# A two-layer decoder trunk on one core: layer 0 in one hand-ordered region, first transfers by k-tile, squares of the norm on GpSimd, retention angles behind the norm

## The chip, the cores and the metric

The kernel runs on one core of one Trainium2 chip. The time is device time of one execution in microseconds. The kernel before took 431.51 us (median of three runs, 431.0 to 431.7); the changed kernel is timed against it on the same chip.

## The reference

A causal trunk of two layers over 256 positions of width 1024, in fp32. Cut to what matters here:

```python
def reference(x, mem, positions, ...):
    cos, sin = rotary_tables(positions, attn_inv)      # 32 frequencies: heads of layer 0
    rcos, rsin = rotary_tables(positions, ret_inv)     # 128 frequencies: retention, layer 1
    mem_n = rms_norm(mem, mem_norm_g)
    x = even_layer(x, mem_n, cos, sin, ...)            # layer 0
    x = odd_layer(x, mem_n, rcos, rsin, ...)           # layer 1
    return rms_norm(x, final_norm_g)

def even_layer(x, ...):
    h = rms_norm(x, norm_g)
    (nq, nkc, nvc, nks, nvs, nkw, nvw, ng, nz, mq, mk, mv, mz, eq, ez) = _split(h @ w_in, EVEN_SPLITS)
    # a_out: sparse attention (compressed, selected, window), b_out: block attention, m_out: memory attention
    y = jnp.concatenate([a_out * jax.nn.silu(nz), b_out * jax.nn.silu(mz), m_out * jax.nn.silu(ez)], axis=-1) @ w_out
    return x + y
```

Layer 1 projects to retention queries, keys, values and gates and to a second memory attention, and maps back in the same way.

## The kernel before

Every product of fp32 matrices is made of three matmuls of a rounded high part and a low part (high by high, high by low, low by high). Weights come from memory in *units* of 128 x 1024 (512 KB; the compression's are 128 x 560), through a ring of six `raw` buffers. For each unit ScalarE casts the high part `whi` (L165), VectorE subtracts the low part `wlo` (L173), both into rings of four; 1.2 us of VectorE and 1.0 us of ScalarE per unit of 1024. TensorE works on the projections one after another: 24 matmuls per unit.

The row norm of `x` is not applied before the projections: x times gain is split (`xh`, `xl`, buffers named `big`), and 1/rms (`rstd0`) is multiplied into the results and the rotary tables later. So the first matmuls need only x and weights, while squares, their sum, and the reciprocal root run beside them.

The start, in order: the first projection (sparse keys, L402 to L411) runs k-tile by k-tile, eight of them. For each, ScalarE casts the weight (`split`, L144) and x (`gain_cast`, L342), VectorE makes the two low parts (L145 and `gain_low`, L346), and TensorE runs six matmuls of 512 columns (L409) into banks s0 and s1. `square(q)` (L399) squares a quarter of x on ScalarE. Then come the compression's projection (four units of 560, 12 matmuls of 280 columns each), the sparse queries (four units of 1024), the sparse gates (`project_turned`, which take banks s0 and s1 again), the block keys, and so on.

Beside the projections run small tasks, written as generators and advanced by `turn()` once per step of a projection (a *slot*, counted from the compression's first). `until(AT[..])` holds a task up to a slot. Four of them matter: `tables` (rotary angles of layer 0, on VectorE), `norms` (adds the squares on GpSimd, L491 and L492; sums over rows by a matmul, L497; reciprocal root by small steps on VectorE, `rsqrt_steps`, L132 to L137; spreads it over the partitions by a matmul, L504; scales the tables on ScalarE, L510 to L518), `tables1` (the angles of layer 1's retention, L483 to L463 on GpSimd, sine and cosine on ScalarE, L465 to L469), and `compressed` (values cast on ScalarE, L747, transposed by TensorE into bank o, L754 and L755).

Inside `tc.manual_schedule(engines=...)` the named engines run their instructions in the order in which the program emits them; outside, a planner orders them. An engine is in order in any case: an instruction that waits holds back all behind it. Before, the start consists of several such regions, some for the sync engine and ScalarE alone, so that the planner may interleave VectorE's, TensorE's and GpSimd's work of neighbouring parts.

## Time and profile before

| | |
|---|---|
| median of three runs | 431.51 us |
| the profiled execution's own time | 431.38 us |
| its span, first to last instruction | 429.6 us |
| TensorE busy | 417.7 us, 97% |
| VectorE busy | 308.1 us, 72% |
| ScalarE busy | 242.3 us, 56% |
| GpSimd busy | 18.1 us, 4%, nearly all between 13 and 33 us |
| granted TensorE clock | 0.998 |

How to read it: PE is TensorE, PEld its weight loads, DVE VectorE, ACT ScalarE, POOL GpSimd; SPq and ACTq are queues that issue transfers. A row of the timeline has start and duration in us, engine, line, operation, what is written and read, and in brackets the idle time before it and who ended it. The busy time is cut into stretches where it is used, since the engines' shares differ between the first 30 us and the rest.

### The profile page before, as it was taken

Reading aid. Unit: us, or ns where it says so; the run is one execution under the profiler, and the core shown is the slowest. Engines: PE = TensorE matmul, PEld = TensorE weight load, DVE = VectorE, ACT = ScalarE, POOL = GpSimd, SP = SyncE. Lnnn points to the kernel's source line nnn. Section 1 sums busy time; section 2 is a strip of 40 time slices with the busy share of each in tenths; the row PEclk is TensorE's granted clock in tenths of the full one; section 3 lists DMA queues with packets and bytes.
Section 4 is the critical chain, followed back from the end, with each engine's and each line's share of the span. In section 5 each row is a group of like instructions: output and inputs, shape, how many; then the busy total and the mean of one; then the engine's idle time right before and its main releaser. Section 6 shows DMA issues by size and latency. Waiting matters only on the chain.

```text
span 429.6 us, 7028 instructions
## 1 busy us (share of the span) xinstructions
PE 417.7 (97%) x2622; PEld 361.1 (84%) x2622; DVE 308.1 (72%) x667; ACT 242.3 (56%) x452; POOL 18.1 (4%) x24
## 2 busy tenths in 40 slices
PE   7889999999999999999999999999999999999994
PEld 5678988777899987879999988889998888888883
DVE  3997988779697585668677674677887467695634
ACT  5759375677876584746356344456444445545703
POOL 0690000000000000000000000000000000000000
PEclk9999999999999999999999999999999999999999
DMA  8786554344666453535444446545454554655102
GB/s 275 269 283 211 199 179 129 135 148 155 215 235 214 133 154 124 163 115 182 156 171 163 153 152 186 196 169 195 148 164 164 178 190 176 205 178 186 69 0 98
DMA packets 21937, 73.18 MB, mean 170 GB/s; under 512 B 2704, under 2 KB 3728, under 8 KB 21904
## 3 DMA queue, kind: packets, MB, share of 16 engines
q1 hardware_dynamic: 21328, 72.04, 50.9%
q10 hardware_dynamic: 576, 0.71, 0.7%
q8 instruction: 20, 0.33, 0.3%
q14 instruction: 13, 0.11, 0.1%
HBM read 71.69 MB, written 1.05 MB: 169 GB/s over the span
## 4 chain that ended last, share of the span: by engine, by line
PE 88%; DVE 7%; DMA 1%; issue 1%; ACT 1%; SPq 0%; DVEq 0%
PE pj L244 23%; PE pj L246 22%; PE pj L245 22%; PE o L116 4%; DVE wlo L173 2%; PE s L116 2%; PE s L323 2%; PE t L323 2%; DMA raw<-in_w 1%; PE s L244 1%; PE s L246 1%; PE s L245 1%; PE tr L244 1%; PE tr L246 1%; PE tr L245 1%
## 5 line engine op out<-in xcount | busy, mean ns | idle before, releaser
L173 DVE TENSOR_TENSOR wlo<-raw,whi 128x1024 fp32r<-128x1024 f32 (+1 forms) x118 | 142.6, 1211 | 62.8 <-ACT whi L165 60.7
L165 ACT CAST whi<-raw 128x1024 fp32r<-128x1024 f32 (+1 forms) x118 | 121.6, 1036 | 91.9 <-PE pj L246 38.2
L244 PE MATMUL pj<-whi,big 128*128 128x512 f32 (+2 forms) x256 | 97.4, 383 | 0.0
L245 PE MATMUL pj<-wlo,big 128*128 128x512 f32 (+2 forms) x256 | 96.2, 376 | 1.1 <-DVE wlo L173 1.1
L246 PE MATMUL pj<-whi,big 128*128 128x512 f32 (+2 forms) x256 | 95.9, 375 | 0.0
L244 PE MATMUL pj<-big,whi 128*128 128x256 f32 x256 | 73.5, 287 | 0.0
L246 PE MATMUL pj<-big,wlo 128*128 128x256 f32 x256 | 72.6, 284 | 0.0
L245 PE MATMUL pj<-big,whi 128*128 128x256 f32 x256 | 72.5, 283 | 0.0
L245 PEld LDWEIGHTS pj<-wlo,big 128*128 128x128 f32 x256 | 48.3, 189 | 9.4 <-DVE wlo L173 1.5
L244 PEld LDWEIGHTS pj<-whi,big 128*128 128x128 f32 x256 | 48.2, 188 | 9.3 <-issue 1.5
L246 PEld LDWEIGHTS pj<-whi,big 128*128 128x128 f32 x256 | 48.2, 188 | 8.7
L244 PEld LDWEIGHTS pj<-big,whi 128*128 128x128 f32 x256 | 49.0, 191 | 1.9 <-issue 1.8
L245 PEld LDWEIGHTS pj<-big,whi 128*128 128x128 f32 x256 | 49.0, 191 | 0.1
L246 PEld LDWEIGHTS pj<-big,wlo 128*128 128x128 f32 x256 | 49.0, 191 | 0.0
L608 ACT ACTIVATE p<-p,mx 128x128 f32<-128x128 f32 (+1 forms) x48 | 21.2, 443 | 4.5 <-DVE mx L595 4.4
L244 PE MATMUL pj<-whi,y 128*128 128x512 f32 x42 | 16.9, 407 | 0.0
L246 PE MATMUL pj<-whi,y 128*128 128x512 f32 x42 | 16.4, 391 | 0.0
L245 PE MATMUL pj<-wlo,y 128*128 128x512 f32 x42 | 16.2, 391 | 0.0
L570 DVE TENSOR_SCALAR p<-p,sm 128x256 f32<-128x256 f32 (+1 forms) x48 | 12.7, 322 | 0.6
L568 ACT ACTIVATE p<-p,sm 128x256 f32<-128x256 f32 (+1 forms) x16 | 7.8, 487 | 7.9 <-DVE sm L564 7.5
L595 DVE CUSTOM_DVE_ANT_0 p<-s,cst 128x128 f32<-128x128 f32 (+1 forms) x24 | 7.1, 353 | 5.5 <-PE s L116 5.5
L409 PE MATMUL s<-whi,big 128*128 128x512 f32 x32 | 9.0, 396 | 2.0 <-ACT big L342 1.6
(349 smaller groups left out, 657.9 us busy)
## 6 DMA issues: line engine op xcount, KB each, us to landing
raw<-in_w SPq DMA_DIRECT2D x91, 512.0 KB, 3.8
raw<-in_wout SPq DMA_DIRECT2D x28, 512.0 KB, 3.9
raw<-in_w SPq DMA_DIRECT2D x4, 280.0 KB, 3.5
v<-in_w SPq DMA_DIRECT2D x2, 512.0 KB, 6.1
raw<-in_memT SPq DMA_DIRECT2D x2, 512.0 KB, 3.8
raw<-in_memtok SPq DMA_DIRECT2D x2, 512.0 KB, 4.6
v<-in_xtok SPq DMA_DIRECT2D x2, 512.0 KB, 5.4
v<-in_grow SPq DMA_DIRECT2D x2, 512.0 KB, 7.2
```

Of the source, the lines that this page charges most:

```text
L116: ins = PE.matmul(out, lhs, rhs, start=start, stop=stop)
L165: S.copy(hi, raw)
L173: V.tensor_tensor(lo, raw, hi.bitcast(F32), ALU.subtract)
L244: PE.matmul(ps, lh, rh, start=start, stop=False, skip_group_check=shared)
L245: PE.matmul(ps, lh, rl, start=False, stop=False, skip_group_check=shared)
L246: return PE.matmul(ps, ll, rh, start=False, stop=stop, skip_group_check=shared)
L323: PE.transpose(b[:, i * P : (i + 1) * P], a, ident)
L409: PE.matmul(ps_k[tok], x[:, kt, tok * P : (tok + 1) * P], w, start=kt == 0 and i == 0, stop=kt == KT - 1 and i == 2)
L568: S.activation(p[:, hh, a], p[:, hh, a], AF.Copy, scale=sm[:, hh, tok : tok + 1])
L570: V.tensor_scalar(p[:, hh, a], p[:, hh, a], sm[:, hh, tok : tok + 1], None, op0=ALU.mult)
L595: V.tensor_tensor_reduce(ps[i][:, hh, a], ss[i][hh][:, a], cpak[:, C_CAUSAL + a.start : C_CAUSAL + a.stop], -1.0, 3e38, ALU.add, ALU.min, ...
L608: S.activation(ps[i][:, hh, a], src, AF.Exp, bias=ms[i][:, hh, tok : tok + 1], scale=-1.0 if causal else 1.0, accum_out=ns[i][:, hh, tok : ...
```

## The change

It rewrites how the first part of the program is ordered.

- The whole of layer 0, from the first transfer to its output projection, becomes one region in which all five engines follow the order of emission.
- The first transfers all go through the sync queue, in the order in which k-tiles use them: weight half, x tile, weight half, and so on; ScalarE's queue keeps only the vector of gains. Each later weight of the first projection (128 x 1024) comes as two transfers. (In the diff, the list of `drive` calls is left out where it only loses its indentation.)
- `square(q)` moves from ScalarE to GpSimd as a product of x with itself, and adds up as it goes; it stands at a k-tile's start instead of one pair later.
- `tables` is advanced by hand behind the first two units of the compression, and no longer interleaved with the last k-tiles.
- `tables1` begins at slot 10 instead of 3, takes its first cast on VectorE, and its sines come at slot 14 instead of 10. The sum of squares comes at slot 3 instead of 5, the compression's steps at 15 and 24 instead of 13 and 22.

```diff
--- before.py
+++ after.py
@@ -31,7 +31,7 @@
 BANKS = {"pj": 3, "tr": 1, "t": 1, "s0": 1, "s1": 1, "o": 1}
 FREE = ("s0", "s1", "t", "tr", "o")
 NEG = -1e30
-AT = {"sum": 5, "spread": 10, "sin": 5, "ret": 3, "rsin": 10, "nsa": 10, "cmp": 13, "blk": 18, "hid": 22, "q": 17}
+AT = {"sum": 3, "spread": 10, "sin": 5, "ret": 10, "rsin": 14, "nsa": 10, "cmp": 15, "blk": 18, "hid": 24, "q": 17}
 MAGIC = 12582912.0
 PI_LO = 3.1415925
 BASE = 16512 + 32 + 416 + 32
@@ -376,40 +376,44 @@
         held[tag] = tl(tag, shape, bufs, dt)
     early.update(held)
     posr = tl("yf", [P, T], 2, I32)
-    with tc.manual_schedule(engines={mybir.EngineType.SP, mybir.EngineType.Activation}):
-        nc.scalar.dma_start(vect, vec)
-        nc.scalar.dma_start(xraw[0][:, 0:2], xT[:, 0:2])
-        load(wraw[0][:, 0:512], w512[2][:, 0:512])
-        load(wraw[0][:, 512:1024], w512[2][:, 512:1024])
-        S.activation(seed, seed, AF.Sin)
-        for q in range(1, 4):
-            load(xraw[q // 2][:, 2 * (q % 2) : 2 * (q % 2) + 2], xT[:, 2 * q : 2 * q + 2])
-            load(wraw[q], w512[2 + q // 2][:, (q % 2) * 1024 : (q % 2 + 1) * 1024])
-        load(cpak, cst)
-        load(posi, pos)
-        load(posr, posrow.to_broadcast([P, T]))
-        for u in range(4):
-            raws.append(load(tl("raw", [P, 1024], NRAW)[:, :560], w280[u // 2][:, u % 2 * 560 : u % 2 * 560 + 560]))
+    order = ExitStack()
+    order.enter_context(tc.manual_schedule(engines=MANUAL))
+    nc.scalar.dma_start(vect, vec)
+    load(wraw[0][:, 0:512], w512[2][:, 0:512])
+    load(xraw[0][:, 0:2], xT[:, 0:2])
+    load(wraw[0][:, 512:1024], w512[2][:, 512:1024])
+    S.activation(seed, seed, AF.Sin)
+    for q in range(1, 4):
+        load(xraw[q // 2][:, 2 * (q % 2) : 2 * (q % 2) + 2], xT[:, 2 * q : 2 * q + 2])
+        for j in range(2):
+            load(wraw[q][:, j * 512 : j * 512 + 512], w512[2 + q // 2][:, (2 * (q % 2) + j) * 512 : (2 * (q % 2) + j + 1) * 512])
+    load(cpak, cst)
+    load(posi, pos)
+    load(posr, posrow.to_broadcast([P, T]))
+    for u in range(4):
+        raws.append(load(tl("raw", [P, 1024], NRAW)[:, :560], w280[u // 2][:, u % 2 * 560 : u % 2 * 560 + 560]))
     wb = bank("t")
     for _ in range(6):
         PE.matmul(wb[:, :256], warm[:, 0:P], warm[:, :256], start=True, stop=True)
 
     def square(q):
 
-        S.activation(squares[q // 2][:, q % 2], xraw[q // 2][:, 2 * (q % 2) : 2 * (q % 2) + 2].rearrange("p k t -> p (k t)"), AF.Square)
-
-    with tc.manual_schedule(engines=MANUAL):
-        for kt in range(KT):
-            q, j = kt // 2, kt % 2
-            wh, wl = split(wraw[q][:, j * 512 : (j + 1) * 512], 512)
-            gain_cast(xraw[q // 2], vect[:, V_G0 : V_G0 + 8], xh, 4 * (q // 2), (kt,))
-            gain_low(xraw[q // 2], vect[:, V_G0 : V_G0 + 8], xh, xl, 4 * (q // 2), (kt,))
-            for i, (x, w) in enumerate(((xh, wh), (xh, wl), (xl, wh))):
-                for tok in range(2):
-                    PE.matmul(ps_k[tok], x[:, kt, tok * P : (tok + 1) * P], w, start=kt == 0 and i == 0,
-                              stop=kt == KT - 1 and i == 2)
-            if q and j:
-                square(q - 1)
+        x = xraw[q // 2][:, 2 * (q % 2) : 2 * (q % 2) + 2].rearrange("p k t -> p (k t)")
+        G.tensor_tensor(squares[q // 2][:, q % 2], x, x, ALU.mult)
+        if q:
+            G.tensor_tensor(squares[0][:, 0], squares[0][:, 0], squares[q // 2][:, q % 2], ALU.add)
+
+    for kt in range(KT):
+        q, j = kt // 2, kt % 2
+        wh, wl = split(wraw[q][:, j * 512 : (j + 1) * 512], 512)
+        gain_cast(xraw[q // 2], vect[:, V_G0 : V_G0 + 8], xh, 4 * (q // 2), (kt,))
+        gain_low(xraw[q // 2], vect[:, V_G0 : V_G0 + 8], xh, xl, 4 * (q // 2), (kt,))
+        for i, (x, w) in enumerate(((xh, wh), (xh, wl), (xl, wh))):
+            for tok in range(2):
+                PE.matmul(ps_k[tok], x[:, kt, tok * P : (tok + 1) * P], w, start=kt == 0 and i == 0,
+                          stop=kt == KT - 1 and i == 2)
+        if j == 0:
+            square(q)
 
     rstd0 = tl("rstd0", [P, 2])
     rb0 = tl("rb", [P, T], 2)
@@ -480,15 +484,13 @@
     def tables1():
 
         yield from until(AT["ret"])
-        G.tensor_copy(kk[:, 64:], posr)
+        V.tensor_copy(kk[:, 64:], posr)
         G.tensor_scalar(ang[:, 64:], kk[:, 64:], cpak[:, C_RFREQ : C_RFREQ + 1], None, op0=ALU.mult)
         yield from angles(G, slice(64, 320))
 
     def norms():
 
         sq = squares[0][:, 0]
-        for part in (squares[0][:, 1], squares[1][:, 0], squares[1][:, 1]):
-            G.tensor_tensor(sq, sq, part, ALU.add)
         G.tensor_tensor(sq[:, :T], sq[:, :T], sq[:, T:], ALU.add)
         yield from until(AT["sum"])
         tag, = yield from take()
@@ -966,34 +968,33 @@
         while len(waiting) > n:
             turn()
 
-    with tc.manual_schedule(engines=MANUAL - {mybir.EngineType.SP}):
-        for u in range(4):
-            fetch()
-            finish()
-            if u == 0:
-                square(3)
+    trig = tables()
+    for u in range(4):
+        fetch()
+        finish()
+        if u < 2:
+            next(trig)
     strict = True
-    with tc.manual_schedule(engines=MANUAL):
-        active.append(tables())
-        active.append(norms())
-        active.append(tables1())
-        free["t"] = free["s0"] = free["s1"] = 1 << 30
...
+    active.append(trig)
+    active.append(norms())
+    active.append(tables1())
+    free["t"] = free["s0"] = free["s1"] = 1 << 30
...
+    crowded = True
+    drive(memory_keys())
...
     def part(acc, tok, c0, n, y, k, wh, wl, start, stop):
@@ -1050,8 +1051,8 @@
         nonlocal acc
         acc = yield from out_project([(yn, 4, 1, ("Yn",)), (yb, 4, 3, ("Yb0", "Yb1")), (ym, 2, 0, ("Ym",))])
 
-    with tc.manual_schedule(engines=MANUAL):
-        drive(first_out())
+    drive(first_out())
+    order.close()
     strict = crowded = False
```

Three places show what this moves. First GpSimd, from its first large operation. v_6 and v_7 hold squares, raw_76 and raw_79 are x; DMAHW names a transfer that is waited for, Pool its own preceding step. Before:

```order
L491 ISA
L491 TENSOR_TENSOR v_6_68<-v_6_68 128x512 [waits Activation_49]
L491 TENSOR_TENSOR v_6_68<-v_6_68,v_7_69 128x512 [waits Activation_49,Pool_49] x2
L492 TENSOR_TENSOR v_6_68<-v_6_68 128x256 [waits Pool_49]
L483 CAST tmp_54_230<-yf_91 128x256 [waits DMAHW4_49]
L484 TENSOR_SCALAR tmp_27_90<-tmp_54_230,cst_65 128x256 [waits DMAHW2_49,Pool_49]
```

Now:

```order
L402 TENSOR_TENSOR v_6_68<-raw_76 128x512 [waits DMAHW2_49]
L402 TENSOR_TENSOR v_6_68<-raw_76 128x512 [waits DMAHW4_49]
L404 TENSOR_TENSOR v_6_68<-v_6_68 128x512 [waits Pool_49]
L402 TENSOR_TENSOR v_7_69<-raw_79 128x512 [waits DMAHW7_49]
L404 TENSOR_TENSOR v_6_68<-v_6_68,v_7_69 128x512 [waits Pool_49]
L402 TENSOR_TENSOR v_7_69<-raw_79 128x512 [waits DMAHW2_49]
L404 TENSOR_TENSOR v_6_68<-v_6_68,v_7_69 128x512 [waits Pool_49]
L494 TENSOR_TENSOR v_6_68<-v_6_68 128x256 [waits Pool_49]
L733 MEMSET kcbd_362 128x30
L735 MEMSET vcr_96 128x256
L488 TENSOR_SCALAR tmp_27_90<-tmp_54_233,cst_65 128x256 [waits DMAHW5_49,DVE_49]
```

Four operations on squares become eight, which wait for transfers of x instead of ScalarE's squares, and the angles' first product (tmp_27) stands behind a VectorE cast.

Second VectorE, from the sixth k-tile's subtract on: wlo are low parts of weights, big_73 of x, posf and tmp the rotary angles of layer 0. Before:

```order
L145 TENSOR_TENSOR wlo_191<-raw_80,whi_190 128x512 [waits Activation_49]
L346 SCALAR_TENSOR_TENSOR big_73<-raw_79,vec_63,big_72 128x256 [waits Activation_49]
L473 CAST posf_233<-pos_64 128x2 [waits DMAHW3_49]
L145 TENSOR_TENSOR wlo_204<-raw_81,whi_203 128x512 [waits DMAHW1_49,Activation_49]
L475 TENSOR_SCALAR tmp_27_90<-cst_65,posf_233 128x32 [waits DMAHW2_49,DVE_49]
L475 TENSOR_SCALAR tmp_27_90<-cst_65,posf_233 128x32
L346 SCALAR_TENSOR_TENSOR big_73<-raw_79,vec_63,big_72 128x256 [waits DMAHW0_49,Activation_49]
L145 TENSOR_TENSOR wlo_216<-raw_81,whi_215 128x512 [waits Activation_49]
L454 TENSOR_SCALAR tmp_54_230<-tmp_27_90 128x64 [waits DVE_49]
L346 SCALAR_TENSOR_TENSOR big_73<-raw_79,vec_63,big_72 128x256 [waits Activation_49]
L455 TENSOR_SCALAR tmp_54_230<-tmp_54_230 128x64 [waits DVE_49]
L173 TENSOR_TENSOR wlo_242<-raw_113,whi_241 128x560 [waits DMAHW5_49,Activation_49]
```

Now:

```order
L145 TENSOR_TENSOR wlo_195<-raw_80,whi_194 128x512 [waits DMAHW1_49,Activation_49]
L346 SCALAR_TENSOR_TENSOR big_73<-raw_79,vec_63,big_72 128x256 [waits Activation_49]
L145 TENSOR_TENSOR wlo_207<-raw_81,whi_206 128x512 [waits DMAHW3_49,Activation_49]
L346 SCALAR_TENSOR_TENSOR big_73<-raw_79,vec_63,big_72 128x256 [waits DMAHW2_49,Activation_49]
L145 TENSOR_TENSOR wlo_221<-raw_81,whi_220 128x512 [waits DMAHW4_49,Activation_49]
L346 SCALAR_TENSOR_TENSOR big_73<-raw_79,vec_63,big_72 128x256 [waits Activation_49]
L173 TENSOR_TENSOR wlo_243<-raw_116,whi_242 128x560 [waits DMAHW0_49,Activation_49]
L477 CAST posf_236<-pos_64 128x2 [waits DMAHW6_49]
L479 TENSOR_SCALAR tmp_27_90<-cst_65,posf_236 128x32 [waits DMAHW5_49,DVE_49]
L479 TENSOR_SCALAR tmp_27_90<-cst_65,posf_236 128x32
L458 TENSOR_SCALAR tmp_54_233<-tmp_27_90 128x64 [waits DVE_49]
L459 TENSOR_SCALAR tmp_54_233<-tmp_54_233 128x64 [waits DVE_49]
```

The five scalar operations of the angles stood between the low parts of the last two k-tiles; they now stand behind all of these and behind the first unit of 560.

Third ScalarE, around the retention sines (trig, 128x256); whi_415 and whi_400 are the fourth weight unit of the queries, whi_444 and whi_434 the first of the gates, s_24 the sparse keys copied out of bank s0, tmp_109 and tmp_112 the compressed values. Before:

```order
L465 ACTIVATE trig_231<-tmp_27_90 128x256 [waits Pool_49]
L466 ACTIVATE trig_232<-tmp_27_90 128x256
L703 ACTIVATE s_74_267<-s_11_74,rstd_53_229 128x256 [waits DVE_49]
L165 CAST whi_415<-raw_270 128x1024 [waits DMAHW4_49,PE_49]
L515 COPY rb_92<-tr_327 128x256 [waits PE_49]
L517 ACTIVATE ctq_234<-ctk_236 128x64
L518 ACTIVATE stq_235<-stk_237 128x128 [waits Activation_49]
L468 ACTIVATE trig_232<-trig_232 128x256 [waits Activation_49]
L469 ACTIVATE trig_232<-trig_232 128x256 [waits Activation_49]
L703 ACTIVATE s_74_267<-s_12_75,rstd_53_229 128x256 [waits DVE_49]
L165 CAST whi_444<-raw_323 128x1024 [waits DMAHW5_49,PE_49]
L747 ACTIVATE tmp_109_467<-pj_268,rstd_53_229 128x128 [waits DVE_49]
```

Now:

```order
L705 ACTIVATE s_74_273<-s_12_75,rstd_53_232 128x256 [waits DVE_49]
L165 CAST whi_434<-raw_318 128x1024 [waits DMAHW0_49,PE_49]
L469 ACTIVATE trig_234<-tmp_27_90 128x256 [waits Pool_49]
L470 ACTIVATE trig_235<-tmp_27_90 128x256
L712 COPY s_24_87<-s_103_439 128x512 [waits PE_49]
L165 CAST whi_460<-raw_346 128x1024 [waits DMAHW1_49]
L472 ACTIVATE trig_235<-trig_235 128x256 [waits Activation_49]
L473 ACTIVATE trig_235<-trig_235 128x256 [waits Activation_49]
L749 ACTIVATE tmp_112_480<-pj_274,rstd_53_232 128x128 [waits DVE_49]
L749 ACTIVATE tmp_112_480<-t_275,rstd_53_232 128x128 [waits DVE_49]
L752 ACT_TABLE_LOAD
L752 ACTIVATE gates_361<-gates_361 128x48
```

Before, the sines stood ahead of the queries' last unit, and the copy of the keys (L710) two rows behind the last one shown. Now they stand behind the gates' first unit and ahead of the copy of the keys, the gates' second unit and the value casts.

More of the change, by code (lines that the diff above doesn't have):

```diff
@@ L967, in started @@
             turn()
-    with tc.manual_schedule(engines=MANUAL - {mybir.EngineType.SP}):
-        for u in range(4):
-            fetch()
-            finish()
-            if u == 0:
-                square(3)
-    strict = True
-    with tc.manual_schedule(engines=MANUAL):
-        active.append(tables())
-        active.append(norms())
-        active.append(tables1())
-        free["t"] = free["s0"] = free["s1"] = 1 << 30
-        sparse_keys(ps_k)
-        drive(compress())
-        drive(sparse_queries())
-        waiting.append(({"qT", "kT"}, sparse_couple(0)))
-        waiting.extend(({f"yn{pr - 1}"}, sparse_couple(pr)) for pr in range(1, 4))
-        drive(sparse_gates())
-        drive(block_keys())
-        drive(block_queries())
-        active.append(making(memory_rows(), "mh"))
-        drive(block_values())
-        active.append(making(memory_scale(), "rbm"))
-        drive(block_gates())
-        waiting.extend(({"mq", "mk", "mvt", "szb", f"yb{c - 1}" if c else "yn3"}, block_couple(c)) for c in range(2))
-        drive(memory_queries())
-        crowded = True
-        drive(memory_keys())
+    trig = tables()
[4 more added lines that the diff above has]
+            next(trig)
+    strict = True
+    active.append(trig)
+    active.append(norms())
+    active.append(tables1())
+    free["t"] = free["s0"] = free["s1"] = 1 << 30
+    sparse_keys(ps_k)
+    drive(compress())
+    drive(sparse_queries())
+    waiting.append(({"qT", "kT"}, sparse_couple(0)))
+    waiting.extend(({f"yn{pr - 1}"}, sparse_couple(pr)) for pr in range(1, 4))
+    drive(sparse_gates())
+    drive(block_keys())
+    drive(block_queries())
+    active.append(making(memory_rows(), "mh"))
+    drive(block_values())
+    active.append(making(memory_scale(), "rbm"))
+    drive(block_gates())
+    waiting.extend(({"mq", "mk", "mvt", "szb", f"yb{c - 1}" if c else "yn3"}, block_couple(c)) for c in range(2))
+    drive(memory_queries())
+    crowded = True
+    drive(memory_keys())
     def part(acc, tok, c0, n, y, k, wh, wl, start, stop):
```

## The prediction

> **What bounds the kernel now.** I read the page first, then the busy time by stretch, then TensorE's waits. The first line is the page's head; the others are stretches of the span, with their length and the busy time (and instructions) of PE, PEld, DVE, ACT and POOL.
>
> ```profile
> span 429.6 us, 7028 instructions
> 5.00:10.00 5.00, 3.36 (x15) 2.51 (x14) 3.08 (x6) 2.90 (x7) 0.00 (x0) 1.00 1.01 371
> 10.00:20.00 10.00, 8.80 (x39) 6.72 (x37) 9.73 (x17) 8.59 (x18) 5.30 (x4) 1.00 0.79 277
> 20.00:30.00 10.00, 8.65 (x60) 7.95 (x61) 9.58 (x23) 4.18 (x9) 9.30 (x10) 1.00 0.86 277
> 60.00:420.00 360.00, 359.67 (x2228) 310.96 (x2227) 255.84 (x556) 202.21 (x370) 0.00 (x0) 1.00 0.49 159
> ```
>
> TensorE is the bound: from 60 us to 420 us it lacks 0.33 us of full. The change removes no matmul, so it can gain only from TensorE's idle time near the start: 1.64 + 1.20 + 1.35 = 4.2 us by these rows. TensorE's waits between 5 and 31 us (line waited for: total, times, longest) name what ends them:
>
> ```profile
> PE s L409 <- ACT big L342: 1.6, 1, 1.6
> PE tr L504 <- DVE rstd L137: 1.1, 1, 1.1
> PE pj L245 <- DVE wlo L173: 1.1, 1, 1.1
> PE s L409 <- DVE big L346: 0.3, 1, 0.3
> ```
>
> The first is the start, waiting for the x tile; the next two are norm chain and weight split, both late on VectorE. VectorE is 96 to 97% busy from 10 to 30 us: this stage sits between two limits, and what loads VectorE there moves the end.
>
> **The first transfers.** Issue to landing of the two weight halves and of the first x tile:
>
> ```profile
> raw<-in_w SPq DMA_DIRECT2D x1, 256.0 KB, 3.6
> raw<-in_w SPq DMA_DIRECT2D x1, 256.0 KB, 4.6
> raw<-in_xT ACTq DMA_DIRECT2D x1, 256.0 KB, 5.4
> 1.18 0.45 ACTq L381 DMA_DIRECT2D raw<-in_xT  x1
> 7.22 0.50 PE L409 MATMUL s<-whi,big 128*128 128x512 f32 x1 [1.64 <-ACT big L342]
> ```
>
> The x tile landed at 1.18 + 5.4 = 6.6 us, TensorE began 0.6 us later. It now stands second on the sync queue; that place's transfer landed after 4.6 us, so by about 5.8, and sooner without x bytes on another queue (not before the first half's 4.3). I take 5.4: a start at 6.0, 1.2 us earlier (bounds 0.8 and 2.3). That is worth something only if the work behind it keeps up.
>
> **The squares on GpSimd.** ScalarE loses its four squares, on which no wait of TensorE hangs; GpSimd gets them, so seven 128x512 operations and one of 256 where four stood. They now run during the first projection, beside VectorE's low parts (subtract L145, scalar-tensor L346), both with two inputs in SBUF. How the two engines get on is in these rows:
>
> ```profile
> 12.55 0.68 DVE L145 TENSOR_TENSOR wlo<-raw,whi 128x512 fp32r<-128x512 f32 x1
> 13.15 0.48 DVE L346 SCALAR_TENSOR_TENSOR big<-raw,vec,big 128x256 fp32r<-128x256 f32 x1
> 13.55 1.27 DVE L473 CAST posf<-pos 128x2 f32<-128x2 int32 x1
> 16.02 0.68 DVE L145 TENSOR_TENSOR wlo<-raw,whi 128x512 fp32r<-128x512 f32 x1
> 26.03 0.66 DVE L137 SCALAR_TENSOR_TENSOR rstd<-rs_t,rstd 128x2 f32<-128x2 f32 x1
> 27.21 0.16 DVE L137 SCALAR_TENSOR_TENSOR rstd<-rs_t,rstd 128x2 f32<-128x2 f32 x1
> 13.45 1.34 POOL L491 TENSOR_TENSOR v<-v 128x512 f32<-128x512 f32 x1 [12.20 <-ACT v L399]
> 15.88 2.01 POOL L491 TENSOR_TENSOR v<-v,v 128x512 f32<-128x512 f32 x1 [1.09 <-ACT v L399]
> 25.93 0.74 POOL L462 TENSOR_TENSOR tmp<-rbm,tmp 128x256 f32<-128x256 f32 x1
> ```
>
> They exclude each other. A two-element cast took 1.27 us while GpSimd added; the same tiny step took 0.66 us beside GpSimd's 25.93 row and 0.16 otherwise, so it was let in at 26.03 + 0.50, 0.14 before that operation's end; and GpSimd's add took 2.01 instead of 1.34 beside a 0.68 us subtract. A GpSimd operation of 512 thus keeps VectorE out for about 1.34 − 0.14 − 0.1 = 1.1 us, one of 256 for 0.5: 7 × 1.1 + 0.5 = 8.2 us. VectorE's pair for a k-tile costs 0.60 + 0.40 (starts 12.55, 13.15, 13.55), eight tiles 8.0 us. Before, GpSimd entered only at 13.45; now 16.2 us of exclusive work must pass between about 5 us and the sum matmul.
>
> I take strict turns, since GpSimd asks again within 0.3 us of letting go, sooner than VectorE's next instruction ends. From 5.65 us (first subtract done): eight turns, 8.2 + 4 × 0.4 + 4 × 0.6 = 12.2, to 17.85; VectorE then stands at k-tile 4's x part (of tiles 0 to 7), done 18.25. TensorE's pace, from its starts:
>
> ```profile
> 16.65 0.84 PE L409 MATMUL s<-whi,big 128*128 128x512 f32 x3
> 17.33 0.61 PE L409 MATMUL s<-wlo,big 128*128 128x512 f32 x2
> 20.23 0.40 PE L245 MATMUL pj<-wlo,big 128*128 128x280 f32 x1 [1.11 <-DVE wlo L173]
> 23.42 0.50 PE L497 MATMUL tr<-ones,v 128*128 128x1 f32 x4
> 26.97 0.40 PE L244 MATMUL pj<-whi,big 128*128 128x512 f32 x1
> 29.65 0.38 PE L504 MATMUL tr<-cst,rstd 128*128 128x128 f32 x1 [1.11 <-DVE rstd L137]
> ```
>
> A matmul every (17.33 − 16.65) / 3 = 0.227 us, six per k-tile: 1.36. Tile 4 ends at 18.25 + 0.45, tiles 5 to 7 take 4.1: 22.8 us. In the run before the next projection went on at 20.23 with one matmul of 0.13 already done, so 20.1. **This term: +2.7 us.** Bounds. If a turn costs the whole 1.34 (and 0.74), the eight turns end at 19.75 and the stage at 24.7: +4.6. If VectorE always goes first, TensorE keeps its pace but waits at the sum, to about 5.05 + 16.2 = 21.25; the change puts 36 short matmuls behind it where 24 stood (0.128 each, from 20.23 to 26.97): 21.25 + 4.6 against 23.42 + 3.1, −0.65. Without any exclusion the stage ends at 6.0 + 10.9 = 16.9: −3.2.
>
> The Trainium skill says it more strictly ("SBUF — State Buffer", "SBUF: two separate sides" and "Who interferes with whom"): a VectorE operation with two SBUF inputs and a GpSimd operation that reads SBUF take one lock, held for the whole instruction, and the other blocks fully. By that rule this term would be the +4.6; the trace's 0.14 us before the end speaks for a little less.
>
> **VectorE's tables behind the last k-tile, and the norm chain.** The cast and four scalar operations for the angles leave the k-tiles. In the run before each waited for GpSimd (13.55 above, two more of 1.3), which made the 0.3 and 1.1 us stalls; these are inside the comparison with 20.1. Afterwards the sum matmul comes at 22.8 + 1.55 = 24.4. Before, 6.2 us passed from it to the spread (23.42 to 29.65), with two GpSimd waits of 0.5 in VectorE's steps that go: 1/rms is there at about 29.6, and the spread, 0.2 + 24.4 + the rest of TensorE's order, is due at about 31.2. Its 1.11 us wait goes: **−1.1 us** (bounds −1.1 and 0). The spread moves from 29.65 to S = 31.2.
>
> **The retention angles.** They start on GpSimd behind a VectorE cast, which stands behind two weight splits after 1/rms:
>
> ```profile
> 27.29 1.23 DVE L173 TENSOR_TENSOR wlo<-raw,whi 128x1024 fp32r<-128x1024 f32 x1
> 28.43 0.68 DVE L135 TENSOR_TENSOR rs_t<-rstd 128x2 f32<-128x2 f32 x1
> 21.35 1.33 POOL L484 TENSOR_SCALAR tmp<-tmp,cst 128x256 f32<-128x256 f32 x1
> 26.76 0.85 POOL L461 TENSOR_SCALAR rbm<-tmp 128x256 f32<-128x256 f32 x1
> 31.42 0.40 POOL L463 TENSOR_SCALAR tmp<-tmp 128x256 f32<-128x256 f32 x1
> L165 ACT CAST whi<-raw 128x1024 fp32r<-128x1024 f32 (+1 forms) x118 | 121.6, 1036 | 91.9 <-PE pj L246 38.2
> 31.85 0.42 ACT L465 ACTIVATE trig<-tmp 128x256 f32<-128x256 f32 x1 [0.92 <-POOL tmp L463]
> 32.48 0.46 ACT L703 ACTIVATE s<-s,rstd 128x256 f32<-128x256 f32 x1
> 36.45 0.37 ACT L747 ACTIVATE tmp<-pj,rstd 128x128 f32<-128x128 f32 x1
> 37.19 0.58 ACT L710 COPY s<-s 128x512 f32<-128x512 f32 x1
> 40.71 0.28 PE L244 MATMUL s<-big,whi 128*128 128x256 f32 x1
> ```
>
> A split takes 1.14 (27.29 to 28.43), so the cast ends 2.6 us after 1/rms, at S + 0.95. The ten GpSimd operations took 10.5 us (21.35 to 31.82). Their shortest forms (0.85, 0.74, 0.40) with gaps of 0.09 make 8.1; I take 9.0, as fewer long two-input operations lie beside them. So they end at S + 9.95. Before, this was S + 2.2, and ScalarE waited 0.92 us for it with nothing urgent behind. Now three things stand behind ScalarE's sine: the copy that frees bank s0 (L712), into which the gate projection writes first; the cast of weight unit 5; and the casts of the compressed values (L749), which TensorE's transposes need half a unit into the gate projection. From the end of GpSimd on: sines 0.63 (31.85 to 32.48), copy 0.58, weight cast 1.04, the two closing angle steps some 0.7 (an estimate from the sines), value casts 0.8 (36.45 to just past 37.19): 3.75, so S + 13.7. The gate projection stood at 40.71 = S + 11.06 with four transposes (0.36) ahead; now they come twelve matmuls of 0.12 into it: due S + 12.4. **+1.3 us** (bounds +0.4 for 8.1 and +2.8 for 10.5), of which the wait at bank s0 is the first part.
>
> **The rest** I cost at nothing: the compression's steps come some matmuls later, covered by a TensorE that has other projections; the residual's three loads fall behind six weight transfers, but are used only after the first layer's output projection; from the projection behind the gates on the order is the same. Uncovered, each would be at most one 0.33 us wait like the one after 60 us.
>
> **Sum,** against the profiled execution's own 431.38 us (span 429.6 and 1.8 around it; the median of the runs is 431.51, 0.03% off): 431.4 + 2.7 − 1.1 + 1.3 = 434.3 us.
>
> **Rivals.** *No exclusion in this stage* (the faster side): VectorE's large subtracts never stand beside a GpSimd add from its start in the run before, only its tiny steps do. Decisive is whether the first k-tile's x part waits for the first square. Then −3.2 − 1.1, and the angles +0.4 to +2.8: S would be 25.4, 428.5 us with 1.5. Against it stands the 2.01 row. Chance 0.24. *VectorE goes first:* the 16.02 subtract started after GpSimd's 15.88 add and still went unhindered. Then −0.65 − 1.1 and +1.3 (0.4 to 2.8): 430.9 us, 430.0 to 432.4. Chance 0.18. *The whole instruction is held:* +4.6 − 1.1 + 1.3: 436.2 us. Chance 0.13. By the skill's rule above this would be the likeliest. *The first tile does not come sooner:* the start stays at 7.2, which costs nothing in the forecast, as turns set the stage; it makes the first rival 1.2 slower.
>
> **How the numbers follow.** The forecast of strict turns has 0.45 and its own range, with the angles' bounds, 433.4 to 435.8. What a measurement here can tell from no change is 0.2%, 0.86 us: 430.65 to 432.4. Faster: 0.24 and a third of 0.18, less what the first rival may lose again: 0.28. Same: half of 0.18 and a little of the forecast: 0.12. Slower: 0.60. The range takes in the first rival nearly whole and the held lock with half a microsecond more: 428.4 to 437.0.
>
> **What would show it.** Right: TensorE's waits for L346 and L145's tiles between 6 and 23 us add to some 4 us; VectorE's means of these lines exceed 0.9 and 0.7 us (0.69 and 0.48 now); GpSimd's 512 operations take over 1.6; the wait before the spread is gone; ScalarE waits several us for GpSimd ahead of its retention sine and TensorE waits once for ScalarE near the gate projection's start. Wrong: VectorE's means unchanged and TensorE dense from 6 us on (first rival), or one wait of 3 us at the sum matmul (second).

## The result, and the profile after

The changed kernel takes **434.64 us** (median of four runs, 434.46 to 434.84); the kernel before took 431.47 us in the same series. The ratio is 1.0075, 95% interval 1.0058 to 1.0093: slower by 3.2 us. A second series of the changed kernel gave 434.44 us, ratio 1.0069 (1.0054 to 1.0084). The profiled execution took 434.46 us, its span 432.7 us (before: 431.38 and 429.6).

The same stretches as before the change, now of the changed kernel (length, then busy time and instructions of PE, PEld, DVE, ACT and POOL; the last three numbers are TensorE's granted clock, the share of the transfer engines and their GB/s):

```profile
5.00:10.00 5.00, 4.80 (x17) 3.07 (x15) 2.87 (x5) 3.04 (x7) 2.58 (x3) 1.00 1.00 354
10.00:20.00 10.00, 7.49 (x26) 4.33 (x27) 10.00 (x11) 5.68 (x13) 8.18 (x8) 1.00 0.69 223
20.00:30.00 10.00, 10.00 (x68) 9.41 (x67) 9.45 (x31) 6.59 (x14) 0.00 (x0) 1.00 0.86 308
30.00:60.00 30.00, 28.59 (x239) 25.34 (x240) 23.28 (x43) 16.42 (x30) 9.86 (x12) 1.00 0.61 210
60.00:420.00 360.00, 359.64 (x2234) 310.43 (x2231) 256.49 (x566) 203.30 (x375) 0.00 (x0) 1.00 0.50 162
```

From 10 to 20 us TensorE falls from 8.80 to 7.49 us with 26 matmul records where 39 stood, while VectorE is full, yet with 11 instructions where it did 17. From 20 to 30 us TensorE's gap of 1.35 us is gone. From 30 to 60 us there is a new one, 1.41 us. TensorE's waits of the changed kernel (line waited for: total, times, longest) name both new ones:

```profile
PE s L413 <- DVE big L346: 1.9, 3, 0.7
PE s L244 <- ACT s L712: 1.2, 1, 1.2
PE s L413 <- DVE wlo L145: 0.5, 2, 0.2
PE s L413 <- ACT big L342: 0.2, 1, 0.2
PE o L757 <- ACT tmp L749: 0.2, 1, 0.2
```

Where the first come from stands in the timelines of VectorE and GpSimd, laid side by side:

```profile
10.28 1.51 DVE L346 SCALAR_TENSOR_TENSOR big<-raw,vec,big 128x256 fp32r<-128x256 f32 x1
11.71 1.52 DVE L145 TENSOR_TENSOR wlo<-raw,whi 128x512 fp32r<-128x512 f32 x1
13.16 1.50 DVE L346 SCALAR_TENSOR_TENSOR big<-raw,vec,big 128x256 fp32r<-128x256 f32 x1
14.58 1.52 DVE L145 TENSOR_TENSOR wlo<-raw,whi 128x512 fp32r<-128x512 f32 x1
18.99 0.68 DVE L145 TENSOR_TENSOR wlo<-raw,whi 128x512 fp32r<-128x512 f32 x1
```
```profile
11.47 1.22 POOL L402 TENSOR_TENSOR v<-raw 128x512 f32<-128x512 f32 x1
12.77 1.61 POOL L404 TENSOR_TENSOR v<-v,v 128x512 f32<-128x512 f32 x1
14.34 1.22 POOL L402 TENSOR_TENSOR v<-raw 128x512 f32<-128x512 f32 x1
17.32 0.80 POOL L494 TENSOR_TENSOR v<-v 128x256 f32<-128x256 f32 x1
```

One GpSimd operation, one of VectorE's, and so on without a break. One k-tile costs VectorE 14.58 − 11.71 = 2.87 us, of which 0.60 + 0.40 is its own work; the two GpSimd operations in it hold it for 0.94 us each on average. As soon as GpSimd is done (17.32 + 0.80), VectorE's subtract takes 0.68 us again. The stage ends like this (changed kernel first, then before):

```profile
22.50 0.29 PE L244 MATMUL pj<-whi,big 128*128 128x280 f32 x1
22.63 0.29 PE L245 MATMUL pj<-wlo,big 128*128 128x280 f32 x1
```
```profile
20.23 0.40 PE L245 MATMUL pj<-wlo,big 128*128 128x280 f32 x1 [1.11 <-DVE wlo L173]
```

The second wait is ScalarE's queue behind the retention sine, with TensorE's row that hangs on it:

```profile
33.78 1.59 POOL L465 TENSOR_SCALAR rbm<-tmp 128x256 f32<-128x256 f32 x1
40.73 0.40 POOL L467 TENSOR_SCALAR tmp<-tmp 128x256 f32<-128x256 f32 x1
41.16 0.42 ACT L469 ACTIVATE trig<-tmp 128x256 f32<-128x256 f32 x1 [5.88 <-POOL tmp L467]
41.79 0.56 ACT L712 COPY s<-s 128x512 f32<-128x512 f32 x1
42.41 0.38 PE L244 MATMUL s<-big,whi 128*128 128x256 f32 x1 [1.24 <-ACT s L712]
```

### The profile page after: what moved, and what is told of

It reads as the page before. It is cut to its first block, busy times and chain, and to the rows that moved or that the text cites. A ratio compares the mean times of both kernels' runs of the same rounds, so it can differ in the third digit from the quotient of the medians.

```text
span 432.7 us, 7033 instructions
## 1 busy us (share of the span) xinstructions
PE 420.6 (97%) x2622; PEld 361.1 (83%) x2622; DVE 308.4 (71%) x668; ACT 240.8 (56%) x448; POOL 21.3 (5%) x27
## 4 chain that ended last, share of the span: by engine, by line
PE 85%; DVE 7%; issue 2%; POOL 2%; DMA 1%; ACT 1%; SPq 0%; DVEq 0%; ACTq 0%; POOLq 0%
PE pj L244 22%; PE pj L246 21%; PE pj L245 21%; PE o L116 4%; PE s L116 2%; PE t L323 2%; DVE wlo L173 2%; PE s L323 2%; DMA raw<-in_w 1%; DVE big L346 1%; PE tr L244 1%; PE tr L245 1%; PE tr L246 1%; PE s L244 1%; PE s L246 1%
## 5 line engine op out<-in xcount | busy, mean ns | idle before, releaser
L145 DVE TENSOR_TENSOR wlo<-raw,whi 128x512 fp32r<-128x512 f32 x8 | 7.7, 963 | 5.6 <-ACT whi L144 5.5
```

The costliest lines, as they stand in the source:

```text
L145: V.tensor_tensor(lo, raw, hi.bitcast(F32), ALU.subtract)
```

## The experiments

My theory: the squares cost what they hold VectorE for in strict turns, and the angles what ScalarE's sine holds back behind it. The rivals: no such exclusion, VectorE going first, a lateness from elsewhere. All times are compared with the kernel before, run in the same series. "The stage" is the first projection. Line numbers shift by a few between kernels; the tile names tell what is what.

| kernel | median, us | ratio to before, 95% | first projection ends |
|---|---|---|---|
| kernel before | 431.47 | 1 | 20.10 |
| changed kernel | 434.64 | 1.0075 (1.0058 to 1.0093) | 22.50 |
| the same again | 434.44 | 1.0069 (1.0054 to 1.0084) | 23.42 |
| squares back on ScalarE | 433.41 | 1.0045 (1.003 to 1.006) | 20.10 |
| sine one slot later | 433.65 | 1.0052 (1.0037 to 1.0067) | 23.43 |
| angles at the old slots | 435.96 | 1.01 (1.0078 to 1.0123) | 23.29 |
| old transfers | 434.31 | 1.0067 (1.0052 to 1.0082) | 22.78 |
| squares back, sine later | 432.19 | 1.0017 (1.0008 to 1.0026) | 19.73 |
| squares made twice | 438.27 | 1.0156 (1.0128 to 1.0185) | 25.38 |
| one input each (leaves the sum of squares out) | 432.30 | 1.001 (0.9998 to 1.0021) | 18.54 |
| early sums, old transfers, sine later | 431.37 | 1.0001 (0.9992 to 1.001) | 20.10 |
| the same, sine behind all casts | 430.25 | **0.9973 (0.9962 to 0.9984)** | 19.91 |
| the same, sums apart | 430.28 | **0.9971 (0.996 to 0.9983)** | 20.07 |
| sums apart, x ahead of the vector | 432.64 | 1.0024 (1.0015 to 1.0033) | 22.37 |

The last column is the start of the compression's first matmul; where its second then waited (before, squares back, squares back with the sine later) it is that second one's start less 0.13.

### The squares back on ScalarE

```diff
-        G.tensor_tensor(squares[q // 2][:, q % 2], x, x, ALU.mult)
-        if q:
-            G.tensor_tensor(squares[0][:, 0], squares[0][:, 0], squares[q // 2][:, q % 2], ALU.add)
+        S.activation(squares[q // 2][:, q % 2], ..., AF.Square)
...
-        if j == 0:
-            square(q)
+        if q and j:
+            square(q - 1)
...
+        for part in (squares[0][:, 1], squares[1][:, 0], squares[1][:, 1]):
+            G.tensor_tensor(sq, sq, part, ALU.add)
...
+        if u == 0:
+            square(3)
```


> The changed kernel with the four squares back on ScalarE and the sums on GpSimd behind them, as before the change; transfers, angles and emission order stay as changed. Strict turns (my theory): GpSimd has three additions beside the first projection instead of seven operations of 512, so TensorE is paced by its own 1.36 us per k-tile from 6.9 us on, 17.8 us, plus some 0.5 to 1 us of turns: the first matmul of the 280-column projection comes at about 18.5 instead of 22.50, the spread at about 27 instead of 30.5, and the time falls by about 3 us to 431.5 (430.3 to 432.5). VectorE's mean for L145 in the stage falls from about 1.2 to under 0.9. No exclusion (rival): what paces the stage is the start, the loads or the clock; the stage's end stays within 0.5 of 22.5 and the time within 0.5 of 434.6. VectorE goes first (rival): the stage's end does not move, only the sum matmul, at most -0.7.

433.41 us, 1.2 us less and not 3. The first matmul of the next projection came at 19.06 us, near the 18.5 expected; but the second waited 0.88 us for the low part of its weights, beside GpSimd's additions, so the stage ended where it stood before the change (20.10), and the spread came at 28.95 and not at 27. TensorE's waits of this kernel show where the rest of the gain goes:

```profile
PE s L244 <- ACT s L711: 2.1, 1, 2.1
PE pj L245 <- DVE wlo L173: 1.1, 2, 0.9
PE s L410 <- ACT big L342: 0.9, 2, 0.5
```

The wait at bank s0 grew from 1.24 to 2.11 us: the matmuls before it came 1.6 us earlier, the angles only 0.7 (their cast stands behind two weight splits of VectorE's). So the two costs are in a row, not beside each other: what the squares give back, the angles keep. "No exclusion" has fallen: 2.4 us of the stage go with the squares.

### The sine one slot later

```diff
-AT = {... "rsin": 14, ...}
+AT = {... "rsin": 15, ...}
```


> The changed kernel with one number moved: the sine of the retention angles comes one turn later (15 for 14), so that on ScalarE the copy that frees bank s0, the cast of the next weight unit and the casts of the compressed values stand ahead of it. My theory (that sine's wait for GpSimd holds the bank): TensorE's waits of 1.24 us at bank s0 and 0.17 us for the value casts go, the gate projection starts at 41.2 instead of 42.4, and the time falls by 1.2 to 1.4 us to 433.3 (433.0 to 433.7). Rival (the gate projection is late by something else, or the wait comes back at the next weight cast or at the gates' exponential): the time stays within 0.4 of 434.6.

433.65 us, 0.8 to 1.0 less than the changed kernel's two series. Neither wait is left in TensorE's list, and the gate projection starts at 41.94 although the first projection ended 0.9 us later in this profile. The lateness came from this one place in ScalarE's order. One thing is not as the expectation has it: the value casts still stand behind the sine (42.63 us; the casts at 43.26 and 43.51), and here they are just in time.

### The angles at the old slots

```diff
-AT = {... "ret": 10, "rsin": 14, ...}
+AT = {... "ret": 3, "rsin": 10, ...}
```


> The changed kernel with the retention angles at the turns they had before the change (3 and 10), so GpSimd works on them beside the chain of the norm again; their first cast stays on VectorE. My theory: the wait at bank s0 (1.24 us) goes, but GpSimd's operations again hold VectorE twice or so in the steps to 1/rms, about 0.5 us each, and TensorE waits up to 1 us before the spread: the two nearly cancel, 434.3 us (433.5 to 434.8). Rival (GpSimd's operations cost the norm's chain nothing): all of the 1.2 to 1.4 us comes off, 433.3 or less. Rival (the angles are not what holds bank s0): the time stays or rises by the spread's wait, up to 435.7.

435.96 us (two runs at 435.05 and 435.35, two at 436.58 and 436.87): both my number and the first rival's fell. The second rival's time is near, but not its reason, since the wait at bank s0 is gone. The angles' start came 5 us earlier, but their sine also moved ahead of other things on ScalarE, so the same mechanism struck elsewhere (timelines of ScalarE and TensorE):

```profile
36.82 0.42 ACT L469 ACTIVATE trig<-tmp 128x256 f32<-128x256 f32 x1 [5.47 <-POOL tmp L467]
37.45 0.46 ACT L705 ACTIVATE s<-s,rstd 128x256 f32<-128x256 f32 x1
37.96 0.66 PE L323 MATMUL s<-cst,rot_a 128*128 128x128 f32 x4 [1.92 <-ACT s L705]
```

A copy that frees a bank stands behind the sine again, and TensorE waits 1.92 us. Behind this wait TensorE's granted clock fell to 0.50 for about 3.4 us (0.94 on average between 30 and 60 us), so the time itself says less than the wait. The steps to 1/rms beside GpSimd cost nothing that TensorE saw.

### The old transfers

```diff
-    load(wraw[0][:, 0:512], ...)
-    load(xraw[0][:, 0:2], xT[:, 0:2])
+    nc.scalar.dma_start(xraw[0][:, 0:2], xT[:, 0:2])
+    load(wraw[0][:, 0:512], ...)
...
+        load(wraw[q], w512[2 + q // 2][:, (q % 2) * 1024 : (q % 2 + 1) * 1024])
```


> The changed kernel with its first transfers as before the change: the first x tile on ScalarE's queue ahead of the weights, the weights of the other pairs of k-tiles in whole transfers of 512 KB. My theory: the x tile lands about 0.35 us later, 6.6 for 6.25, the first square and so the chain of turns start that much later, and the time rises by 0.3 us to 434.9 (434.4 to 435.3). Rival (the order of transfers is worth the 1.2 us that I gave to the start): 435.8 or more. Rival (whole transfers hold back later k-tiles): VectorE or ScalarE waits for a weight tile in the stage and the time rises by more than 0.5.

434.31 us: no difference (434.64 and 434.44), and just under the 434.4 to 435.3 expected. The first matmul came at 7.08 us for 6.88. Neither the 1.2 us rival nor the late-weights rival is seen.

### The squares made twice, and with one input

```diff
+        for _ in range(2):
             G.tensor_tensor(squares[q // 2][:, q % 2], x, x, ALU.mult)
```


> The changed kernel with each square made twice on GpSimd, four more operations of 512 beside the first projection. Strict turns with what the trace of the changed kernel shows (two GpSimd operations and one pair of VectorE's in 2.87 us, so 0.94 us of VectorE's time for each): twelve turns instead of eight, VectorE stands at k-tile 6 when they end at about 23.9, and the stage ends at about 26 instead of 22.5: +3.5 us (3.0 to 4.0), about 438. No exclusion, or VectorE first (rivals): the stage's end moves by less than 0.5 us, and only the sum matmul may be later.

The stage's end moved from 22.50 to 25.38 us: 2.9, just under the 3.0 to 4.0 expected. The turns went on, at 2.63 to 2.87 us for a k-tile. (The two runs took 437.08 and 439.45 us; a wait at bank s0 of 2.42 us and a granted clock of 0.50 for some 3.4 us behind it are in the profile of the longer one.)

```diff
-        G.tensor_tensor(squares[q // 2][:, q % 2], x, x, ALU.mult)
-        if q: G.tensor_tensor(squares[0][:, 0], squares[0][:, 0], squares[q // 2][:, q % 2], ALU.add)
+        G.tensor_scalar(squares[q // 2][:, q % 2], x, 1.0, None, op0=ALU.max)
+        if q: G.tensor_scalar(squares[0][:, 0], squares[q // 2][:, q % 2], 1.0, None, op0=ALU.mult)
```


> The changed kernel with the same number of GpSimd operations of the same size in the same places, but each square and each addition of squares replaced by an operation with one input from SBUF (the larger of x and 1; a copy); this leaves the sum of squares out of the computation, so the output is scaled wrongly. If only operations with two inputs exclude VectorE's: L145 and L346 keep their 0.69 and 0.48 us, TensorE is dense from 7 us on, the stage ends at 18 to 18.5 instead of 22.5, and the time falls by about 2 us or, as the wait at bank s0 grows, by 1.2. If any GpSimd operation that reads SBUF excludes them: the turns stay, L145 and L346 take over 1.2 us on the average beside GpSimd, and the stage ends within 0.7 of 22.5.

432.30 us (430.94 to 432.73; the profile, of a run of 432.65, has a granted clock of 0.50 for some 3.4 us behind a wait at bank s0 of 1.75 us). The stage ended at 18.54 us with no wait for VectorE in it. GpSimd is as busy as ever (groups of GpSimd's and VectorE's instructions from 5 to 20 us: count, busy us, mean ns; then VectorE's timeline):

```profile
L402 POOL TENSOR_SCALAR v<-raw 128x512 f32<-128x512 f32 x4 | 7.5, 1880 | 5.6 <-DMA raw<-in_xT 5.6
L145 DVE TENSOR_TENSOR wlo<-raw,whi 128x512 fp32r<-128x512 f32 x8 | 6.3, 786 | 5.0 <-ACT whi L144 5.0
L346 DVE SCALAR_TENSOR_TENSOR big<-raw,vec,big 128x256 fp32r<-128x256 f32 x8 | 4.9, 609 | 1.2 <-ACT big L342 1.2
```
```profile
8.87 0.83 DVE L346 SCALAR_TENSOR_TENSOR big<-raw,vec,big 128x256 fp32r<-128x256 f32 x1
10.62 1.10 DVE L145 TENSOR_TENSOR wlo<-raw,whi 128x512 fp32r<-128x512 f32 x1
```

Five of GpSimd's first six operations held one VectorE instruction each, for 0.35 to 0.41 us (0.83 for 0.48, 1.10 for 0.69) and not for 0.94, though they lasted longer themselves; the first held none. So it is not "any GpSimd operation that reads SBUF" that costs 0.94 us: operations with two inputs on GpSimd's side cost much more than those with one. The instruction differs as well (TENSOR_SCALAR for TENSOR_TENSOR), and no run separates the two. Why one input still costs 0.35 us is open.

### Towards a version that beats both

The first two edits together:

> The changed kernel with both suspected costs taken out: the squares back on ScalarE with the sums behind them, and the retention sine one turn later. My theory: the two are separate terms. With the squares alone back, TensorE still waited 2.11 us at bank s0 and 0.17 us for the value casts; both go, and the time is 433.4 - 2.2 = 431.2 us (430.6 to 431.8), level with the kernel before. Rival (the gate projection's lateness comes from elsewhere, or the wait reappears behind the sine at the weight casts): 432.4 or more.

432.19 us, a microsecond more than expected. The wait at bank s0 is gone. ScalarE's order is that of the run with the sine one slot later, with the value casts behind the sine; but TensorE now reaches their transposes at 40.47 us instead of 43.38, while the sine comes only 1.7 us sooner (40.96 for 42.63). TensorE's waits show the 1.2 us that is missing:

```profile
PE o L756 <- ACT tmp L748: 1.2, 1, 1.2
```

The rival's second half, a wait that reappears on ScalarE, holds, at the value casts and not at the weight casts.

```diff
-        G.tensor_tensor(squares[q // 2][:, q % 2], x, x, ALU.mult)
+        S.activation(squares[q // 2][:, q % 2], ..., AF.Square)
         if q: G.tensor_tensor(squares[0][:, 0], squares[0][:, 0], squares[q // 2][:, q % 2], ALU.add)
-        if j == 0:
+        if kt in (1, 3, 5, 6):
             square(q)
```

This edit of the changed kernel, with the old transfers and the sine at slot 15:

> A version meant to beat both kernels: the changed kernel with the squares on ScalarE behind k-tiles 1, 3, 5 and 6, each addition on GpSimd right behind its square (so that it lies beside the first projection, where VectorE's 1.0 us per k-tile has 0.36 us to spare), the first transfers as before the change, and the retention sine one turn later. My theory: three additions hold VectorE 0.94 us each, about what it has to spare; the first projection ends at about 18.2 us, the 0.9 us wait for the first split behind it and the wait at bank s0 go, the spread comes at about 27, and the time is 429.5 us (428.5 to 430.5), faster than before the change. Rival (additions beside the projection cost TensorE what they cost behind it): 431 to 432.

431.37 us, level with before, so the rival's time and not the 429.5 expected; the first projection ended at 20.10 us and not at 18.2. The 0.9 us wait for the first split is gone and the same wait for the value casts (1.21 us) stands, with 0.23 and 0.49 us in the first projection beside the additions.

```diff
-AT = {... "rsin": 15, ...}
+AT = {... "rsin": 16, ...}
```


> The version with early sums and old transfers, whose sine still stood ahead of the casts of the compressed values on ScalarE (TensorE waited 1.21 us for them), with that sine one more turn later (16 for 15), so behind these casts. My theory: the wait goes and nothing takes its place, 431.4 - 1.2 = 430.2 us (429.7 to 430.7), now faster than the kernel before. Rival (the wait reappears behind the sine, at the gates' exponential or the weight casts): 431 or more.

430.25 us, as expected to the tenth: **1.2 us faster than the kernel before**, ratio 0.9973 (0.9962 to 0.9984). Every wait of TensorE's over 0.2 us in the whole run, but for the one at its warm-up (the third comes behind 60 us and stands in the kernel before too):

```profile
PE s L411 <- DVE wlo L145: 0.5, 1, 0.5
PE s L411 <- ACT big L342: 0.5, 1, 0.5
PE tr L323 <- DVE p L570: 0.3, 1, 0.3
PE s L411 <- DVE big L346: 0.3, 1, 0.3
PE o L116 <- PE s L246: 0.3, 1, 0.3
```

ScalarE's timeline at the sine:

```profile
40.26 0.42 ACT L467 ACTIVATE trig<-tmp 128x256 f32<-128x256 f32 x1 [3.31 <-POOL tmp L465]
```

ScalarE still waits 3.31 us for GpSimd; now no wait of TensorE's hangs on what stands behind it.

```diff
-    nc.scalar.dma_start(vect, vec)
     nc.scalar.dma_start(xraw[0][:, 0:2], xT[:, 0:2])
+    nc.scalar.dma_start(vect, vec)
-        if kt in (1, 3, 5, 6):
+        if kt in (1, 3, 4, 6):
```


> The same with the third square two k-tiles earlier (behind k-tiles 1, 3, 4 and 6), so that the additions lie further apart, and with the x tile issued ahead of the small vector on ScalarE's queue. My theory: the additions no longer fall back to back, so TensorE's two waits of 0.23 and 0.49 us beside them shrink by some 0.5 us, and the x tile lands about 0.4 us sooner: 429.3 us (428.8 to 430.2). Rival (three additions hold VectorE wherever they lie, and the x cast then waits for the vector instead): the same as the version it is made from, 430.2.

432.64 us, 2.4 us slower than the version it is made from. The x tile was there in time; the vector of 52 KB behind it on the queue was not (its transfer with the median time from issue to landing; then ScalarE's timeline):

```profile
vec<-in_vec ACTq DMA_DIRECT2D x1, 52.0 KB, 7.4
```
```profile
8.68 0.51 ACT L342 ACTIVATE big<-raw,vec 128x256 fp32r<-128x256 f32 x1 [2.24 <-DMA vec<-in_vec]
```

In the version that this one is made from it landed in 3.7 us, ahead of x. In this run TensorE has no wait beside the additions, so one more run took the second edit alone:

```diff
-        if kt in (1, 3, 5, 6):
+        if kt in (1, 3, 4, 6):
```

> The version that measured 430.25 us with one number moved: the third square comes behind k-tile 4 instead of 5, so that GpSimd's three additions no longer lie back to back; the vector stays ahead of the x tile. In the run with the vector behind the x tile TensorE began 2.3 us late for want of the vector, but the additions at this place cost it no wait at all. My theory: the waits of 0.32 and 0.51 us in the first projection go and 429.4 us is left (429.0 to 429.9). Rival (in that run they cost nothing only because VectorE had been given 2 us of lead): 430.2.

430.28 us: the rival holds. The two waits only changed their places (0.63 and 0.47 us, 1.1 in all, for 0.32 and 0.51): three additions hold VectorE for what they hold it, and it has not that much to spare. What hid them in the run before was a slow TensorE. Behind its wait of 2.98 us for the vector its granted clock was 0.50 up to some 12.4 us (a stretch of that run; the clock is the third number from the end), and the stage's first ten matmuls took 3.87 us instead of 2.39:

```profile
10.00:11.00 1.00, 1.00 (x4) 0.80 (x3) 0.82 (x2) 0.87 (x3) 0.00 (x0) 0.50 1.05 416
```

So VectorE had its lead from the slow matmuls, and the 1.5 us that they lost are about what the hidden waits would have cost.

### The changed kernel again

> The changed kernel itself again. Three kernels with the same instructions in the first projection ended it at 22.50, 23.43 and 23.29 us. If the order in which VectorE and GpSimd take their turns is settled anew in each execution by when the first tiles land, this profile may show either pattern, TensorE waiting 0.7 and 0.25 us in turn or 0.45 and 0.50, with the stage's end between 22.4 and 23.5; the time is 434.6 (434.2 to 435.2).

With no edit at all, this profile shows the other pattern, waits of 0.45 and 0.49 us in turn, and the first projection ends at 23.42 for 22.50 us. The span is 432.8 for 432.7: of the 0.9 us the shorter wait at bank s0 (0.93 for 1.24 us) gave back 0.3, and another 0.45 came back at the transposes at 126 us.

VectorE's rows tell the patterns apart. Here L346 takes 1.26 us and L145 1.77, where the first profile has 1.51 and 1.52. Read by the order in which the operations end, an addition holds VectorE for 1.0 to 1.1 us and a square for 0.8; in the first profile the additions stand ahead of L346, here ahead of L145. So the 0.94 us is a mean of two kinds, and the squares made twice, which added four of the cheaper kind, had to cost less than four times 0.94.

## Why the prediction was right, point by point

**The start: wrong in size, with little effect.** I had the x tile land at 5.4 us by the time of the weight in that place of the queue. ScalarE's cast of it came at 6.32 and TensorE's first matmul at 6.88, so 0.34 us sooner than before and not 1.2. The step "that place's transfer landed after 4.6 us" failed: the transfers of x on the sync queue took 6.2 us (transfers of the changed kernel; GpSimd's timeline, where the first square waits for the tile):

```profile
raw<-in_xT SPq DMA_DIRECT2D x4, 256.0 KB, 6.2
```
```profile
6.31 1.04 POOL L402 TENSOR_TENSOR v<-raw 128x512 f32<-128x512 f32 x1 [5.06 <-DMA raw<-in_xT]
```

It cost the forecast little: the old transfers give the same time. It enters only in that the turns began later, as the next point says.

**Squares: +2.7 forecast, +2.4 measured** (22.63 against 20.23 us at the same matmul), 3.3 in the other profile. Strict turns are shown, by the rows above, by the undoing (−2.4 us of the stage) and by the doubling (+2.9). Off in size: a turn holds VectorE for 0.94 us on average, not 1.1; the seven operations are 1.1 us cheaper. On the other side the first square began 0.7 us later than 5.65, with the x tile, and GpSimd stood idle for 1.03 us more before the second; unbroken turns begin at 8.38 us at the earliest. The list of signs held but for two (VectorE's and GpSimd's groups from 5 to 20 us; two rows of TensorE):

```profile
L145 DVE TENSOR_TENSOR wlo<-raw,whi 128x512 fp32r<-128x512 f32 x8 | 7.7, 963 | 5.6 <-ACT whi L144 5.5
L346 DVE SCALAR_TENSOR_TENSOR big<-raw,vec,big 128x256 fp32r<-128x256 f32 x7 | 6.7, 956 | 0.6 <-ACT big L342 0.6
L402 POOL TENSOR_TENSOR v<-raw 128x512 f32<-128x512 f32 x4 | 4.8, 1198 | 6.1 <-DMA raw<-in_xT 6.1
```
```profile
14.71 1.20 PE L413 MATMUL s<-whi,big 128*128 128x512 f32 x4 [0.69 <-DVE big L346]
19.29 1.08 PE L413 MATMUL s<-whi,big 128*128 128x512 f32 x4
```

VectorE's means are over 0.9 and 0.7 us. GpSimd's operations of 512 were to take over 1.6 us; the squares take 1.20 on average, and only the additions reach 1.61 to 1.73. TensorE's waits for the two add to 2.4 us and not to some 4. The loss itself is larger, 22.50 − 6.88 − 10.9 = 4.7 us, because a listed wait is shorter than what it costs: four matmuls go from 19.29 to 20.21 in a dense row, 0.92 us, and from 14.71 to 16.16 with a wait behind them, 1.45; that is 0.53 lost, and the list has 0.25 for it.

By the Trainium skill's rule ("SBUF — State Buffer", "SBUF: two separate sides") the lock is held for the whole instruction, and this term would have been +4.6. The stage did not take that, since two operations hold VectorE for 1.87 us and not for two times 1.34. Whether the lock itself is shorter than the instruction stays open: rows of 1.22 to 1.61 us contain GpSimd's own wait for VectorE, and the one square that began with VectorE idle lasted 1.04 us (6.31 above).

**The spread: −1.1 forecast.** The wait of 1.11 us is gone, and TensorE is full from 20 to 30 us. What that is worth comes with the sum.

**The angles: +1.3 forecast, +1.4 in listed waits** (1.24 at bank s0 and 0.17 at the value casts), and 0.8 to 1.0 us came back when the sine was moved. The forecast's own working has a slip: from its rows the transposes were due at S + 11.06 − 0.36 + 12 × 0.12 = S + 12.1 and not S + 12.4, and the term is then +1.6. The chain on GpSimd took 31.35 to 41.13, 9.8 us for the 9.0 taken, inside its bounds of 8.1 and 10.5: two operations stood beside VectorE's and stretched to 1.59 and 1.68 us. It began at the spread + 0.83 (forecast 0.95). ScalarE's wait of 5.88 us was the "several us" of the list.

**The sum.** By the listed waits it is 2.4 − 1.1 + 1.4 = 2.7, and the span grew by 3.1. As a listed wait falls short of its cost, TensorE's lag at the same instruction is the better measure. Its first and its second group of L323, before and then after the change:

```profile
34.33 0.60 PE L323 MATMUL s<-cst,rot_a 128*128 128x128 f32 x4
45.03 0.60 PE L323 MATMUL t<-cst,rot_a 128*128 128x128 f32 x4
```
```profile
35.10 0.60 PE L323 MATMUL s<-cst,rot_a 128*128 128x128 f32 x4
47.68 0.60 PE L323 MATMUL t<-cst,rot_a 128*128 128x128 f32 x4
```

The lag is 2.40 us at the end of the stage, 0.77 at the first group, behind the spread, and 2.65 at the second, behind the gate's wait and the value casts. So the three terms are +2.4, −1.6 (0.24 of it in the compression, before the spread) and +1.9, for +2.7, −1.1 and +1.3. The last two are off by 0.5 and 0.6 us in opposite directions; that the sum came within 0.35 us of the measured 434.64 is in part luck.

The rest, 0.4 us, is in no wait before 60 us. Some 0.3 of it appears at the transposes that stand at 123.12 us before and 125.94 us after: TensorE lags 2.6 us in front of them and 2.9 behind. What holds them is open.

**The rivals.** The stated range, 428.4 to 437.0, holds the times of all three rivals that have one, so a time inside it says little; what decides are the rows and the runs. Without exclusion the time would have been 428.5; VectorE first, 430.9; the whole instruction held, 436.2. Neither of the first two patterns is in any of the profiles with the squares on GpSimd as two-input operations. What I had not seen: the first and third terms are in a row. A shorter stage alone moves the wait to bank s0. The forecast was the sum of terms that each were right only as long as the others stood.

## What to carry to other kernels

Elementwise work with two inputs does not belong on GpSimd beside a VectorE that is near the bound: here eight operations cost 2.4 us, while ScalarE, which had given up the squares, was idle 4.3 of the 10 us from 10 to 20. An activation that waits for a slow engine belongs behind everything on ScalarE that frees a bank or feeds TensorE; whether it does harm depends on when TensorE arrives, so look the place up again after every edit: the two runs with 1.2 us at the value casts have the order on ScalarE that cost nothing in an earlier run, where TensorE came later. And before adding up the terms of several edits, ask which of them lie on one chain: the two undone alone gave 1.2 and 0.9 us, both together 2.3, and undone to the end, with the sums moved, 4.3.
